# Turning four tiles of a token mixer by VectorE block transposes and DMAs instead of TensorE transposes

## The chip, the cores and the metric

The kernel runs on one core of one Trainium2 chip. The metric is the device time of one execution in microseconds (us), the median over several runs. "Before" is the kernel without the change.

## The reference

Two layers of a decoder trunk act on `x`, 256 tokens of 1024 values, in f32. Each layer is a SwiGLU feed-forward, a mixer with three gated branches, and a second feed-forward, each between two RMS norms. Cut to the mixer, the part that the change touches:

```python
u, bg, cg, q, kv, nsa_g, q_mem, merge_g = jnp.split(h @ w_in, points, axis=-1)
y_conv = bg * short_conv(cg * u, conv_w)                  # 512 channels, width 3 over tokens
...                                                       # y_nsa: native sparse attention
q_m = q_mem.reshape(b, s, MEM_HEADS, MEM_HEAD_DIM)        # 4 heads of 128, 256 memory tokens
s_m = jnp.einsum('bshd,bmhd->bhsm', q_m, mkv[:, :, 0]) * (MEM_HEAD_DIM ** -0.5)
p_m = jax.nn.softmax(s_m, axis=-1)
y_mem = jnp.einsum('bhsm,bmhd->bshd', p_m, mkv[:, :, 1]).reshape(b, s, 512)
g_conv, g_nsa, g_mem = jnp.split(jax.nn.sigmoid(merge_g), 3, axis=-1)
merged = g_conv * (y_conv @ w_br_conv) + g_nsa * (y_nsa @ w_br_nsa) + g_mem * (y_mem @ w_br_mem)
return merged @ w_out
```

## The kernel before

**Streams and steps.** The 256 tokens are two tiles of 128 (`t` = 0 and 1), and each tile is a Python generator, a "stream", that yields after each step of TensorE work. The program runs the two streams in turn, and between them background tasks (attention, compression, memory). A counter `now` counts steps; `later(d, fn)` emits `fn` d steps on. A step of a 512-column projection (`halves`) is six matmuls of 512 columns, and there are 816 steps. The text is thus written in a certain order, and a scheduler then sets the order on each engine from that order, from its table of instruction costs (the lines with `TRN2Spec` change it) and from the buffers that are free; only SP, which issues the weight loads, keeps the order of the text. What an engine got in its list it runs strictly in that order.

**Precision.** Every f32 product is three matmuls in a rounded f32 format: high by high, high by low, low by high. So each weight tile `raw` (128x1024, from a DMA) is split: ACT rounds it to `whi` (L333), DVE subtracts to get `wlo` (L334). Units are split up to `AHEAD` = 4 steps before TensorE needs them, into 8 buffers. Activations are split in the same manner (`evac_split`).

**Turning.** TensorE contracts over partitions, so what a projection leaves as tokens by channels must be turned to channels by tokens before the next one. The kernel has two ways.

- `transpose4` (L441): four TensorE transposes of 128x128 against the identity into one PSUM bank `pt`, which ACT and DVE then read and split. The normed x, the attention's keys and queries, the memory queries `qms`, the convolution's input `v` and gate `bs`, and the gated sum `merged` (in halves of 512 columns) go this way.
- `turn` and `turn_beside`: DVE transposes all 32x32 blocks of a tile (`blocks`, L451), and after `AWAY` = 1 step GpSimd (POOL) issues four DMAs (`moved`, L457) that carry the blocks to their partitions. `wait` steps later ACT and DVE split `moved` (L474, L475). For the block transposes to give the right pieces, the columns are to lie "by lanes", every fourth column together. The feed-forward's gates do it while they read PSUM (`lanes_in`, L661, L663, L668). The SwiGLU products, the attention probabilities, the memory's keys and the memory itself go this way.

**The mixer**, per tile and layer: projections for keys and values, queries, memory queries (`mem_query`), u, C and B (`conv_part`, `conv_out`), then for each branch in `ORDER` = conv, mem, nsa, and for each half n of the 1024 columns: a gate projection whose tanh is `gth`, the branch product `br`, and DVE's gated sum into `merged0` or `merged1` (L1435, L1437, L1438). After the last branch `transpose_half(0)` is emitted `HALF` = 5 steps on, `transpose_half(1)` during the output product `y`, whose unit k takes channels 128k to 128k+127 of the sum; k = 0 to 3 need half 0.

`later(CONV, turn)`, `later(BS, turn)` and `later(QM, turn)` put the transposes of v, bs and qms 7, 4 and 2 steps behind the reads of PSUM. `mem_attention` of both tiles is queued when tile 1's query is turned.

Of the kernel before, what the change touches and what calls it, by code (L numbers as in the profile page):

```python
# [32 lines left out]
P = 128  # L33
# [23 lines left out]
LANES = 4  # L57
NORM_B, NORM_C = 1, 1
AWAY, SPLIT, RETURN = 1, 11, 6
MSTEP, MWAIT = (5, 11), 3  # L60
ABREAST = 6
SECOND_HALF = 1
CONV, BS, CMP, ZC, QS_0, QS_1, QM, PC, YM = 7, 4, 6, 2, 2, 6, 2, 3, 1
ATT_A, ATT_B, ATT_C, ATT_D, ATT_T = 1, 3, 2, 6, 8
EARLY, RAMP, SCALES, STAGED, SETUP = 6, 10, 5, 8, 30
DRAINED = 4
PACE, PACE_1, PACED = 9, 8, ("nsa", "memory")

RUNS = {"ffn1_w_out": 64, "ffn2_w_out": 64, "w_mix_out": 64, "w_branch_conv": 64, "w_branch_mem": 64}
PRE = ("ffn1_norm_pre", "mix_norm_pre", "ffn2_norm_pre", "mem_norm")  # L70
# [73 lines left out]
def f32(ap):  # L144
    return ap.bitcast(F32)
# [19 lines left out]
def program(tc, nc, pools, a, out, plan):  # L165
# [278 lines left out]

    def turn(src, n, finish, wait):
        f = n // 4
        make = gtile if n > 512 else ttile
        blocks = make("blocks")  # L450
        nc.vector.transpose(blocks[:, :n], view(src, 0, [[32, 4], [P, n // P], [1, 32]]))  # L451
        moved = []

        def away():
            moved.append(make("moved"))
            for q in range(4):
                nc.gpsimd.dma_start(moved[0][:, q * f:(q + 1) * f],  # L457
                                    blocks[q * 32:(q + 1) * 32, :n].rearrange("j (p f) -> j p f", p=4))
# [754 lines left out]
    def mem_query(t, l, ps, r):  # L1213
        S = shared[l]
        qs = ttile("qms")
        nc.scalar.activation(qs[:, :512], ps, AF.Copy, scale=r[3])

        def turn():
            pt = transpose4(qs, 0)
            qT = gtile("qmT", F32R)  # L1220
            evac_split(qT[:, 0:512], qT[:, 512:1024], pt)
            S["qm"][t] = qT
            if t == 1:
                S["ymT"] = [gtile("ymemh", F32R), gtile("ymeml", F32R)]
                for u in range(2):
                    add(("memory", l), mem_attention(l, u), True)

        later(QM, turn)

    def mem_attention(l, u):  # L1230
        S = shared[l]
# [49 lines left out]
    def conv_part(t, l, u_s, c_ps, r):  # L1281
        S = shared[l]
        v = ttile("v")
        nc.vector.scalar_tensor_tensor(v[:, :512], c_ps, r[0], u_s[:, :512], op0=OP.mult, op1=OP.mult)
        cT = ttile("cT")

        def turn():
            pt = transpose4(v, 0)
            vT = tp.tile([P, 4, 130], F32, name="vT", tag="tmp")
            if t == 0:  # L1290
                nc.gpsimd.memset(vT[:, :, 0:2], 0.0)
                S["carry"] = sp.tile([P, 4, 2], F32, name="carry", bufs=1)
            else:
                nc.gpsimd.tensor_copy(vT[:, :, 0:2], S["carry"])
            nc.scalar.copy(vT[:, :, 2:130], pt.rearrange("p (c s) -> p c s", c=4))
            if t == 0:
                nc.gpsimd.tensor_copy(S["carry"], vT[:, :, 128:130])
            base = l * 48 + 32
            for c in range(4):
                dst = cT[:, c * P:(c + 1) * P]  # L1300
                w = [convT[:, base + 4 * i + c:base + 4 * i + c + 1] for i in range(3)]
                nc.scalar.activation(dst, pt[:, c * P:(c + 1) * P], AF.Copy, scale=w[2])
# [3 lines left out]
        later(CONV, turn)
        return cT

    def conv_out(cT, b_ps, r, put):
        bs = ttile("bs")  # L1310
        nc.scalar.activation(bs[:, :512], b_ps, AF.Copy, scale=r[1])

        def turn():
            pt = transpose4(bs, 0)
            nc.vector.tensor_tensor(cT[:, :512], cT[:, :512], pt, op=OP.mult)
            y = gtile("yconv", F32R)
            nc.scalar.copy(y[:, 0:512], cT[:, :512])
            nc.vector.tensor_sub(y[:, 512:1024], cT[:, :512], f32(y[:, 0:512]))
            put(y)

        later(BS, turn)

    def branch(yT, name, l, n0):
        ps = bank("br")
# [36 lines left out]
    def mixer(t, l):  # L1361
        S = shared[l]
        hT, r = yield from prenorm(t, "mix_norm_pre", l)

        def columns(c0, n=512):
            return halves(hT, "w_mix_in", l, [(c0, n)])

        ps = yield from columns(2048)
        kv_first(t, l, ps, r)
        ps = yield from halves(hT, "w_mix_in", l, [(2560, P), (2816, 12), (2688, P), (2828, 12)], (0, P, 140, 268))  # L1370
        kv_second(t, l, ps, r)

# [22 lines left out]
        nc.scalar.activation(u_s[:, :512], ps, AF.Copy, scale=r[0])  # L1395
# [4 lines left out]
        conv_out(cT, ps, r, made.append)  # L1400
        merged = [ttile(f"merged{n}") for n in range(2)]
        mh, ml = gtile("mThi", F32R), gtile("mTlo", F32R)

        def transpose_half(n):
            sl = slice(n * 512, (n + 1) * 512)
            evac_split(mh[:, sl], ml[:, sl], transpose4(merged[n], 0))

        for b in ORDER:
            name = ("w_branch_conv", "w_branch_nsa", "w_branch_mem")[b]
            ths = []  # L1410

            def gates(n):
                pg = yield from columns(3352 + b * 1024 + n * 512)
                ths.append(ttile("gth"))
                nc.scalar.activation(ths[n][:, :512], pg, AF.Tanh, scale=r[1])

            if b == 0:
                yield from gates(0)
                yield from gates(1)
            for n in range(2):  # L1420
                if b != 0:
                    yield from gates(n)
                th = ths[n]
# [10 lines left out]
                if b == ORDER[0]:  # L1434
# [89 lines left out]
```

## Time and profile before

| | |
|---|---|
| median of 3 runs (lowest to highest) | 1190.03 us (1189.97 to 1190.53) |
| the profiled execution: its time, its span | 1190.01 us, 1188.3 us |
| granted TensorE clock over the span | 0.999 |
| busy: PE, DVE, ACT, POOL | 1177.2, 891.7, 755.9, 177.2 us |
| TensorE transposes of qms, v, bs, merged | 16, 16, 16, 32 |
| DMAs `moved<-blocks` | 176, 4.3 us from issue to landing for one of 128 KB |
| mixer of layer 0, mixer of layer 1 | about 197 to 421 us, about 788 to 1007 us |

The span runs from the first to the last instruction; 1.7 us of the execution lie outside it. PE is TensorE's matmul side, PEld its weight loads, DVE VectorE, ACT ScalarE, POOL GpSimd. L with a number is a line of the kernel before. A matmul's listed duration runs from its start to its modelled end, and matmuls overlap, so what one costs is read from the distance of starts.

### The profile page before, as it was taken

Reading aid. Unit: us, or ns where it says so; the run is one execution under the profiler, and the core shown is the slowest. Engines: PE = TensorE matmul, PEld = TensorE weight load, DVE = VectorE, ACT = ScalarE, POOL = GpSimd, SP = SyncE. Lnnn points to the kernel's source line nnn. Section 1 sums busy time; section 2 is a strip of 40 time slices with the busy share of each in tenths; the row PEclk is TensorE's granted clock in tenths of the full one; section 3 lists DMA queues with packets and bytes.
Section 4 is the critical chain, followed back from the end, with each engine's and each line's share of the span. In section 5 each row is a group of like instructions: output and inputs, shape, how many; then the busy total and the mean of one; then the engine's idle time right before and its main releaser. Section 6 shows DMA issues by size and latency. Waiting matters only on the chain.

```text
span 1188.3 us, 16619 instructions
## 1 busy us (share of the span) xinstructions
PE 1177.2 (99%) x5777; PEld 1032.5 (87%) x5777; DVE 891.7 (75%) x1130; ACT 755.9 (64%) x1217; POOL 177.2 (15%) x333
## 2 busy tenths in 40 slices
PE   9999999999999999999999999999999999999997
PEld 7888888888988888888888888889888888888886
DVE  6867757798998786676577677588899977767753
ACT  6655836888885565555465565469889655655541
POOL 4001301411120020011011011014012200110100
PEclk9999999999999999999999999999999999999999
DMA  7787875776678767777767678757767687587771
GB/s 258 253 256 240 276 261 154 228 240 192 194 231 216 247 185 221 222 235 230 228 184 230 215 229 270 240 141 242 232 178 229 198 231 229 178 250 213 234 223 63
DMA packets 133764, 260.64 MB, mean 219 GB/s; under 512 B 15694, under 2 KB 36848, under 8 KB 133680
## 3 DMA queue, kind: packets, MB, share of 16 engines
q1 hardware_dynamic: 124048, 235.11, 63.7%
q0 software_dynamic: 9600, 24.47, 7.6%
q8 instruction: 45, 0.74, 0.3%
q14 instruction: 39, 0.32, 0.1%
q10 hardware_dynamic: 32, 0.01, 0.0%
HBM read 235.42 MB, written 2.10 MB: 200 GB/s over the span
## 4 chain that ended last, share of the span: by engine, by line
PE 95%; ACT 2%; DVE 1%; issue 1%; DMA 0%; POOL 0%; SPq 0%; DVEq 0%; POOLq 0%; ACTq 0%
PE acc L410 35%; PE acc L396 9%; PE acc L397 9%; PE acc L398 9%; PE y L398 7%; PE y L396 7%; PE y L397 7%; PE pt L441 2%; PE br L396 2%; PE br L398 2%; PE br L397 2%; ACT whi L333 1%; PE s L1070 1%; DVE wlo L334 0%; PE om L1268 0%
## 5 line engine op out<-in xcount | busy, mean ns | idle before, releaser
L334 DVE TENSOR_TENSOR wlo<-raw,whi 128x1024 fp32r<-128x1024 f32 (+2 forms) x441 | 529.0, 1211 | 186.0 <-ACT whi L333 182.0
L333 ACT CAST whi<-raw 128x1024 fp32r<-128x1024 f32 (+2 forms) x441 | 452.6, 1040 | 255.2 <-PE acc L410 116.1
L457 POOL DMA_DIRECT2D moved<-blocks x176 | 95.8, 563 | 644.6 <-DVE blocks L451 368.9
L410 PE MATMUL acc<-wlo,hThi 128*128 128x512 f32 x640 | 191.6, 380 | 0.0
L410 PE MATMUL acc<-whi,hTlo 128*128 128x512 f32 x640 | 191.4, 380 | 0.0
L410 PE MATMUL acc<-whi,hThi 128*128 128x512 f32 x640 | 191.4, 381 | 0.0
L396 PE MATMUL acc<-whi,hThi 128*128 128x512 f32 (+1 forms) x480 | 182.8, 381 | 0.0
L397 PE MATMUL acc<-wlo,hThi 128*128 128x512 f32 (+1 forms) x480 | 179.3, 374 | 0.3 <-DVE wlo L334 0.2
L398 PE MATMUL acc<-whi,hTlo 128*128 128x512 f32 (+1 forms) x480 | 178.9, 373 | 0.0
L410 PEld LDWEIGHTS acc<-whi,hTlo 128*128 128x128 f32 x640 | 121.2, 189 | 17.3 <-DVE hTlo L513 0.4
L410 PEld LDWEIGHTS acc<-wlo,hThi 128*128 128x128 f32 x640 | 121.1, 189 | 17.0 <-DVE wlo L334 0.3
L410 PEld LDWEIGHTS acc<-whi,hThi 128*128 128x128 f32 x640 | 120.7, 189 | 16.6
L396 PE MATMUL y<-whi,turnhi 128*128 128x512 f32 x352 | 133.8, 380 | 0.0
L397 PE MATMUL y<-wlo,turnhi 128*128 128x512 f32 x352 | 133.7, 380 | 0.0
L398 PE MATMUL y<-whi,turnlo 128*128 128x512 f32 x352 | 133.7, 380 | 0.0
L398 PEld LDWEIGHTS acc<-whi,hTlo 128*128 128x128 f32 x480 | 90.9, 189 | 11.6
L397 PEld LDWEIGHTS acc<-wlo,hThi 128*128 128x128 f32 x480 | 91.1, 190 | 10.9 <-DVE wlo L334 0.9
L396 PEld LDWEIGHTS acc<-whi,hThi 128*128 128x128 f32 x480 | 91.1, 190 | 10.3
L398 PEld LDWEIGHTS y<-whi,turnlo 128*128 128x128 f32 x352 | 66.7, 189 | 9.2
L397 PEld LDWEIGHTS y<-wlo,turnhi 128*128 128x128 f32 x352 | 66.7, 189 | 9.2
L396 PEld LDWEIGHTS y<-whi,turnhi 128*128 128x128 f32 x352 | 66.7, 189 | 9.2
L475 DVE TENSOR_TENSOR turnlo<-moved,turnhi 128x1024 fp32r<-128x1024 f32 (+1 forms) x42 | 49.1, 1168 | 26.8 <-ACT turnhi L474 26.4
(307 smaller groups left out, 1449.6 us busy)
## 6 DMA issues: line engine op xcount, KB each, us to landing
raw<-in_ffn_w_in_dram SPq DMA_DIRECT2D x159, 512.0 KB, 4.7
raw<-in_w_mix_in_dram SPq DMA_DIRECT2D x96, 512.0 KB, 4.5
raw<-in_ffn_w_out_dram SPq DMA_DIRECT2D x88, 512.0 KB, 4.6
moved<-blocks POOLq DMA_DIRECT2D x144, 128.0 KB, 4.3
raw<-in_ffn_w_in_dram SPq DMA_DIRECT2D x34, 256.0 KB, 4.0
raw<-in_w_mem_kv_dram SPq DMA_DIRECT2D x16, 512.0 KB, 4.6
raw<-in_w_mix_out_dram SPq DMA_DIRECT2D x16, 512.0 KB, 4.9
raw<-in_cmp_k_w_dram SPq DMA_DIRECT2D x8, 512.0 KB, 4.6
```

Of the source, the lines that this page charges most:

```text
L333: pinned(nc.scalar.copy(hi[:, c0:c1], raw[:, c0:c1]))
L334: pinned(nc.vector.tensor_sub(lo[:, c0:c1], raw[:, c0:c1], f32(hi[:, c0:c1])))
L396: nc.tensor.matmul(ps, lhsT=xh, rhs=wh, start=start, stop=False, skip_group_check=skip)
L397: nc.tensor.matmul(ps, lhsT=xh, rhs=wl, start=False, stop=False, skip_group_check=skip)
L398: nc.tensor.matmul(ps, lhsT=xl, rhs=wh, start=False, stop=stop, skip_group_check=skip)
L410: pinned(nc.tensor.matmul(ps[j][:, :n], lhsT=hT[x2][:, k], rhs=moving(w, j * n, n), start=(k == 0 and i == 0), stop=(k == 7 and i == 2)))
L441: pinned(nc.tensor.transpose(pt[:, j * P:(j + 1) * P], src[:, c0 + j * P:c0 + (j + 1) * P], ident))
L457: nc.gpsimd.dma_start(moved[0][:, q * f:(q + 1) * f], blocks[q * 32:(q + 1) * 32, :n].rearrange("j (p f) -> j p f", p=4))
L475: nc.vector.tensor_sub(lv, mv, f32(hv))
L1070: nc.tensor.matmul(s3[:, i], lhsT=QT[:, g * 2 + u, i], rhs=pairs(KT[j][:, var * 2 + g], 0, 256), start=(i == 0 and j == 0), stop=(i == 1 a ...
```

## The change

Four tiles change from the first way of turning to the second, and the delays and one cost of the scheduler are set anew.

- **v and bs** (convolution's input and gate): the reads of PSUM (`by_lane`) and the writes put the columns by lanes, `turn(..., laned=True)` transposes blocks on DVE and moves them by four DMAs of 64 KB; the convolution reads `vT`, which ACT copies from `moved`, in place of the PSUM bank; the gate multiplies `moved` instead of `pt`.
- **qms**: `turn_two` writes the block transposes of both tiles into one buffer and moves both with four DMAs of 128 KB, once tile 1's query is there; the split and the start of the memory attention of both tiles follow `QM` steps later.
- **merged, half 0**: tanh, gating and branch product of half 0 are read and written by lanes; after the last branch `move_half` block-transposes it, and the split comes `MERGED` = 11 steps later or ahead of the output product's first unit. Half 1 stays with TensorE.
- **Numbers**: ACT costs 1.05 times as much in the scheduler's table; the constants below.

```diff
+TRN2Spec.CYCLE_T[mybir.EngineType.Activation] *= 1.05
+MERGED = 11
-CONV, BS, CMP, ZC, QS_0, QS_1, QM, PC, YM = 7, 4, 6, 2, 2, 6, 2, 3, 1
-ATT_A, ATT_B, ATT_C, ATT_D, ATT_T = 1, 3, 2, 6, 8
+CONV, BS, CMP, ZC, QS_0, QS_1, QM, PC, YM = 10, 8, 8, 3, 2, 6, 9, 5, 1
+ATT_A, ATT_B, ATT_C, ATT_D, ATT_T = 1, 2, 2, 6, 8
-PACE, PACE_1, PACED = 9, 8, ("nsa", "memory")
+PACE, PACE_1, PACED = 10, 8, ("nsa", "memory")
...
-    def turn(src, n, finish, wait):
+    def turn(src, n, finish, wait, laned=False):
-        nc.vector.transpose(blocks[:, :n], view(src, 0, [[32, 4], [P, n // P], [1, 32]]))
+        nc.vector.transpose(blocks[:, :n], src[:, :n] if laned else view(src, 0, [[32, 4], [P, n // P], [1, 32]]))
...
+    def by_lane(ap, n=512):
+        return view(ap, 0, [[1, 4], [4, n // 4]])
+
+    def turn_two(S, key, t, src, finish, wait):
+        if t == 0:
+            S[key] = gtile("blocks")
+        blocks = S[key]
+        nc.vector.transpose(view(blocks, t * P, [[256, 4], [1, P]]), view(src, 0, [[P, 4], [1, P]]))
+        if t == 0:
+            return
...
+                nc.gpsimd.dma_start(moved[0][:, q * 256:(q + 1) * 256],
+                                    blocks[q * 32:(q + 1) * 32, :].rearrange("j (p f) -> j p f", p=4))
+        later(AWAY, away)
+        later(wait, lambda: finish([view(moved[0], u * P, [[32, 4], [256, 4], [1, 32]]) for u in range(2)]))
...
     # mem_query
-        nc.scalar.activation(qs[:, :512], ps, AF.Copy, scale=r[3])
-            pt = transpose4(qs, 0)
-            evac_split(qT[:, 0:512], qT[:, 512:1024], pt)
-        later(QM, turn)
+        nc.scalar.activation(view(qs, 0, [[P, 4], [1, P]]), by_lane(ps), AF.Copy, scale=r[3])
+                evac_split(quarters(qT[:, 0:512], 4), quarters(qT[:, 512:1024], 4), mv[u])
+        turn_two(S, "qb", t, qs, ready, QM)
...
     # conv_part
-            pt = transpose4(v, 0)
-            nc.scalar.copy(vT[:, :, 2:130], pt.rearrange("p (c s) -> p c s", c=4))
-                nc.scalar.activation(dst, pt[:, c * P:(c + 1) * P], AF.Copy, scale=w[2])
-        later(CONV, turn)
+            nc.scalar.copy(view(vT, 2, [[130, 4], [32, 4], [1, 32]]), mv)
+                nc.scalar.activation(dst, vT[:, c, 2:130], AF.Copy, scale=w[2])
+        turn(v, 512, lambda mv: shifted(mv, t, cT), CONV, True)
...
     # conv_out
-            pt = transpose4(bs, 0)
-            nc.vector.tensor_tensor(cT[:, :512], cT[:, :512], pt, op=OP.mult)
-        later(BS, turn)
+            nc.vector.tensor_tensor(quarters(cT[:, :512], 4), quarters(cT[:, :512], 4), mv, op=OP.mult)
+        turn(bs, 512, lambda mv: gated(mv, cT, put), BS, True)
...
     # mixer
+        def move_half():
+            def place(mv):
+                if not placed:
+                    placed.append(True)
+                    nc.scalar.copy(quarters(mh[:, 0:512], 4), mv)
+                    nc.vector.tensor_sub(quarters(ml[:, 0:512], 4), mv, f32(quarters(mh[:, 0:512], 4)))
+            moved = turn(merged[0], 512, place, MERGED, True)
+            return lambda: place(turned_view(moved[0], 512))
...
+                    if b == 0:
+                        yield ("until", lambda: len(made) > 0)
...
                 if b == ORDER[2] and n == 0:
-                    later(HALF, lambda: transpose_half(0))
+                    first_half = move_half()
...
         def between(k):
+            if k == 0:
+                first_half()
             if k == SECOND:
                 transpose_half(1)
```

Of the built programs' instructions, 64 TensorE transposes go (16 each of qms, v and bs, 16 of the 32 of merged), 16 DVE block transposes come (`STREAM_TRANSPOSE`, four each), and 56 DMAs come on POOL's queue (48 of 64 KB, 8 of 128 KB). The number of ACT instructions stays, and SP's list is the same. The steps of the two streams fall as before.

**TensorE, end of layer 0's mixer.** The half-0 transposes of tile 0's sum stand among the gate products before:

```order
L397 MATMUL acc<-wlo,hThi 128x512
L398 MATMUL acc<-whi,hTlo 128x512
L441 MATMUL pt<-ident,merged_3091 128x128 x4
L396 MATMUL acc<-whi,hThi 128x512
L397 MATMUL acc<-wlo,hThi 128x512
```

and now the gate products go straight over into the output product `y`, with no transposes there:

```order
L399 MATMUL acc<-wlo,hThi 128x512
L400 MATMUL acc<-whi,hTlo 128x512
L398 MATMUL y_4201<-whi,mThi 128x512
L399 MATMUL y_4201<-wlo,mThi 128x512
L400 MATMUL y_4201<-whi,mTlo 128x512
L398 MATMUL y_4202<-whi,mThi 128x512
```

What moved: the four `merged` transposes have left TensorE's list. Between the last matmul of the branch product that completes tile 0's half 0 and the first `y` stand 78 matmuls of 512 columns now.

**DVE, the same place.** Before (from the sum of tile 0's half 0 on; `_3091` and `_3208` are the half-0 sums of tiles 0 and 1):

```order
L1438 TENSOR_TENSOR merged_3091<-merged_3091,gth 128x512
L334 TENSOR_TENSOR wlo<-raw,whi 128x1024 x2
L1437 SCALAR_TENSOR_TENSOR gth<-gth,br 128x512
L1438 TENSOR_TENSOR merged_3208<-merged_3208,gth 128x512
L334 TENSOR_TENSOR wlo<-raw,whi 128x1024 x2
L433 TENSOR_TENSOR mTlo<-pt,mThi 128x512
```

Now (`_3052` and `_3143` are the half-0 sums of the two tiles):

```order
L1477 SCALAR_TENSOR_TENSOR gth<-gth,br 128x512
L1034 TENSOR_TENSOR yf<-o,yf 64x512
L1478 TENSOR_TENSOR merged_3052<-merged_3052,gth 128x512
L336 TENSOR_TENSOR wlo<-raw,whi 128x1024
L1043 TENSOR_TENSOR ynsa<-yf,ynsa 128x512
L453 STREAM_TRANSPOSE blocks<-merged_3052 128x512
L336 TENSOR_TENSOR wlo<-raw,whi 128x1024
L1477 SCALAR_TENSOR_TENSOR gth<-gth,br 128x512
L336 TENSOR_TENSOR wlo<-raw,whi 128x1024
L1478 TENSOR_TENSOR merged_3143<-merged_3143,gth 128x512
L336 TENSOR_TENSOR wlo<-raw,whi 128x1024
L453 STREAM_TRANSPOSE blocks<-merged_3143 128x512
```

What moved: a block transpose of each tile has come in; behind these rows stand one `wlo` and then `mTlo<-moved,mThi` of tile 0, which waits for the four DMAs, with further `wlo` behind it.

**DVE, the convolution of layer 0.** Before, tile 0's `v` is followed by attention work and its turn is TensorE's:

```order
L1284 SCALAR_TENSOR_TENSOR v<-acc,rs,us 128x512
L1192 TENSOR_TENSOR sc<-sc,nmc 128x128
L451 STREAM_TRANSPOSE blocks<-pm 128x1024
L1195 TENSOR_REDUCE smc<-sc 128x8
L334 TENSOR_TENSOR wlo<-raw,whi 128x1024
```

and now:

```order
L1307 SCALAR_TENSOR_TENSOR v<-acc,rs,us 128x512
L435 TENSOR_TENSOR qmT<-moved,qmT 128x512
L453 STREAM_TRANSPOSE blocks<-v 128x512
L1191 TENSOR_TENSOR vlo<-vs,vf 32x64
L1194 TENSOR_TENSOR vst<-vf,gmask 64x128
```

What moved: the memory queries' low parts (`qmT`), before done right after each query, now come here, both tiles together, from `moved`, and `v` has its block transpose on DVE.

More of the change, by code (lines that the diff above doesn't have):

```diff
@@ L465, in turned_view, with away @@
         return view(moved, 0, [[32, n // P], [n // 4, 4], [1, 32]])
+    def by_lane(ap, n=512):
[7 more added lines that the diff above has]
+            return
+        moved = []
+        def away():
+            moved.append(gtile("moved"))
+            for q in range(4):
+                nc.gpsimd.dma_start(moved[0][:, q * 256:(q + 1) * 256],
+                                    blocks[q * 32:(q + 1) * 32, :].rearrange("j (p f) -> j p f", p=4))
+        later(AWAY, away)
+        later(wait, lambda: finish([view(moved[0], u * P, [[32, 4], [256, 4], [1, 32]]) for u in range(2)]))
     def quarters(ap, c):
@@ L1215, in mem_query, with ready @@
         qs = ttile("qms")
-        nc.scalar.activation(qs[:, :512], ps, AF.Copy, scale=r[3])
-        def turn():
-            pt = transpose4(qs, 0)
-            qT = gtile("qmT", F32R)
-            evac_split(qT[:, 0:512], qT[:, 512:1024], pt)
[L1222 to L1226, printed above, removed]
-        later(QM, turn)
+        nc.scalar.activation(view(qs, 0, [[P, 4], [1, P]]), by_lane(ps), AF.Copy, scale=r[3])
+        def ready(mv):
+            for u in range(2):
+                qT = gtile("qmT", F32R)
+                evac_split(quarters(qT[:, 0:512], 4), quarters(qT[:, 512:1024], 4), mv[u])
+                S["qm"][u] = qT
+            S["ymT"] = [gtile("ymemh", F32R), gtile("ymeml", F32R)]
+            for u in range(2):
+                add(("memory", l), mem_attention(l, u), True)
+        turn_two(S, "qb", t, qs, ready, QM)
     def mem_attention(l, u):
@@ L1283, in conv_part, with shifted @@
         v = ttile("v")
-        nc.vector.scalar_tensor_tensor(v[:, :512], c_ps, r[0], u_s[:, :512], op0=OP.mult, op1=OP.mult)
+        lane = lambda ap: view(ap, 0, [[P, 4], [1, P]])
+        nc.vector.scalar_tensor_tensor(lane(v), by_lane(c_ps), r[0], lane(u_s), op0=OP.mult, op1=OP.mult)
         cT = ttile("cT")
-        def turn():
-            pt = transpose4(v, 0)
+        S.setdefault("cT", [None, None])[t] = cT
+        def shifted(mv, t, cT):
             vT = tp.tile([P, 4, 130], F32, name="vT", tag="tmp")
@@ L1301, in turn, with conv_out, gated @@
                 w = [convT[:, base + 4 * i + c:base + 4 * i + c + 1] for i in range(3)]
[L1302 removed]
+                nc.scalar.activation(dst, vT[:, c, 2:130], AF.Copy, scale=w[2])
                 nc.vector.scalar_tensor_tensor(dst, vT[:, c, 1:129], w[1], dst, op0=OP.mult, op1=OP.add)
                 nc.vector.scalar_tensor_tensor(dst, vT[:, c, 0:128], w[0], dst, op0=OP.mult, op1=OP.add)
[L1306 removed]
+        turn(v, 512, lambda mv: shifted(mv, t, cT), CONV, True)
         return cT
[L1309 removed]
+    def conv_out(t, l, cT, b_ps, r, put):
+        S = shared[l]
         bs = ttile("bs")
[L1311 to L1315 removed]
+        nc.scalar.activation(view(bs, 0, [[P, 4], [1, P]]), by_lane(b_ps), AF.Copy, scale=r[1])
+        def gated(mv, cT, put):
+            nc.vector.tensor_tensor(quarters(cT[:, :512], 4), quarters(cT[:, :512], 4), mv, op=OP.mult)
             y = gtile("yconv", F32R)
@@ L1394, in mixer @@
         u_s = ttile("us")
-        nc.scalar.activation(u_s[:, :512], ps, AF.Copy, scale=r[0])
+        nc.scalar.activation(view(u_s, 0, [[P, 4], [1, P]]), by_lane(ps), AF.Copy, scale=r[0])
         ps = yield from columns(1024)
@@ L1399, in mixer @@
         made = []
-        conv_out(cT, ps, r, made.append)
+        conv_out(t, l, cT, ps, r, made.append)
         merged = [ttile(f"merged{n}") for n in range(2)]
@@ L1406, in transpose_half @@
             evac_split(mh[:, sl], ml[:, sl], transpose4(merged[n], 0))
+        placed = []
+        def move_half():
[6 more added lines that the diff above has]
+            return lambda: place(turned_view(moved[0], 512))
         for b in ORDER:
@@ L1414, in gates @@
                 ths.append(ttile("gth"))
-                nc.scalar.activation(ths[n][:, :512], pg, AF.Tanh, scale=r[1])
+                nc.scalar.activation(view(ths[n], 0, [[P, 4], [1, P]]) if n == 0 else ths[n][:, :512],
+                                     by_lane(pg) if n == 0 else pg, AF.Tanh, scale=r[1])
             if b == 0:
@@ L1433, in mixer @@
                 dst = merged[n][:, :512]
-                if b == ORDER[0]:
+                if n == 0:
+                    lane = lambda ap: view(ap, 0, [[P, 4], [1, P]])
+                    if b == ORDER[0]:
+                        nc.vector.scalar_tensor_tensor(lane(dst), lane(th), 1.0, by_lane(pb), op0=OP.add, op1=OP.mult)
+                    else:
+                        nc.vector.scalar_tensor_tensor(lane(th), lane(th), 1.0, by_lane(pb), op0=OP.add, op1=OP.mult)
+                        nc.vector.tensor_add(dst, dst, th[:, :512])
+                elif b == ORDER[0]:
                     nc.vector.scalar_tensor_tensor(dst, th[:, :512], 1.0, pb, op0=OP.add, op1=OP.mult)
```

## The prediction

> **What bounds the kernel.** I read the page's first part, then the chain that ended last, then TensorE's waits, then stretches of the two mixers.
>
> ```profile
> span 1188.3 us, 16619 instructions
> ...
> PE 1177.2 (99%) x5777; PEld 1032.5 (87%) x5777; DVE 891.7 (75%) x1130; ACT 755.9 (64%) x1217; POOL 177.2 (15%) x333
> ...
> PE 95%; ACT 2%; DVE 1%; issue 1%; DMA 0%; POOL 0%; SPq 0%; DVEq 0%; POOLq 0%; ACTq 0%
> ```
>
> TensorE is busy 99% of the span, and 95% of the chain is TensorE's own work, so the time is nearly the sum of what TensorE issues. All its waits over 0.15 us:
>
> ```profile
> PE pt L441 <- DMA x<-in_x_dram: 1.4, 1, 1.4
> PE idle L205 <- DVE idle L200: 1.1, 1, 1.1
> PE z L1111 <- DVE wlo L334: 1.0, 2, 0.6
> PE pt L441 <- POOL kd L905: 0.4, 1, 0.4
> PE z L1109 <- DVE FHL L1100: 0.2, 1, 0.2
> PE acc L397 <- DVE wlo L334: 0.2, 1, 0.2
> ```
>
> The first two belong to the start. Inside a mixer what ends last, when TensorE waits at all, is a late `wlo`, the split of a weight. Where that is near, the stretches show (length, then busy time of PE, PEld, DVE, ACT, POOL); layer 0's mixer first, then layer 1's:
>
> ```profile
> 220.00:260.00 40.00, 38.20 (x228) 32.85 (x227) 35.65 (x47) 36.06 (x67) 14.97 (x21) 1.00 0.79 248
> 260.00:360.00 100.00, 100.00 (x535) 89.05 (x534) 93.52 (x155) 85.45 (x202) 15.73 (x31) 1.00 0.68 206
> 360.00:420.00 60.00, 60.00 (x287) 52.47 (x287) 45.73 (x48) 32.75 (x40) 2.17 (x4) 1.00 0.81 232
> ```
>
> ```profile
> 800.00:860.00 60.00, 59.84 (x363) 53.81 (x362) 51.66 (x72) 54.86 (x129) 15.88 (x24) 1.00 0.76 234
> 860.00:950.00 90.00, 90.00 (x475) 79.94 (x474) 85.89 (x139) 74.12 (x161) 18.73 (x35) 1.00 0.68 202
> ```
>
> TensorE idles 1.80 us in 220 to 260 and 0.16 us in 800 to 860. From 260 to 360 it never idles though DVE is 94% full, and from 360 on DVE has a quarter of its time free. So the mixers have two close seconds: DVE, and early on ACT.
>
> **Removed: 64 TensorE transposes.** Their price is the distance of starts, not the listed duration:
>
> ```profile
> 388.97 0.60 PE L441 MATMUL pt<-ident,merged 128*128 128x128 f32 x4
> 389.33 0.46 PE L396 MATMUL acc<-whi,hThi 128*128 128x512 f32 x1
> 389.63 0.38 PE L397 MATMUL acc<-wlo,hThi 128*128 128x512 f32 x1
> ```
>
> ```profile
> 288.70 0.44 PE pt L441 x4
> ...
> 297.14 0.88 PE pt L441 x8
> ...
> 389.14 0.44 PE pt L441 x4
> ...
> 431.13 95.19 PE acc L410 x441
> ```
>
> In the chain 441 matmuls of 512 columns take 95.19 us, 0.216 each. In the timeline the four transposes hold back the next matmul by 0.36 us, and the matmul behind them takes 0.30 us to the next start in place of 0.216, 0.44 us in all, which is what the chain gives for a set of four (0.88 for eight). Sixteen sets go, all on the path: 16 x 0.44 = 7.04 us. Nothing comes to TensorE's list.
>
> **Added on DVE: 16 block transposes of 512 columns.** No row has that size; the same operation on 1024 and 768 columns, and other operations on 512:
>
> ```profile
> L334 DVE TENSOR_TENSOR wlo<-raw,whi 128x1024 fp32r<-128x1024 f32 x431 | 521.7, 1222 | 184.3 <-ACT whi L333 182.0 <-PE acc L410 1.1
> ...
> L668 DVE TENSOR_TENSOR wide<-th,acc 128x512 f32<-128x512 f32 x40 | 27.5, 688 | 2.9
> L451 DVE STREAM_TRANSPOSE blocks<-wide 128x1024 f32<-128x1024 f32 x16 | 19.8, 1239 | 0.0
> ...
> L451 DVE STREAM_TRANSPOSE blocks<-wide 128x768 f32<-128x768 f32 x8 | 7.8, 975 | 0.1
> ...
> L433 DVE TENSOR_TENSOR mTlo<-pt,mThi 128x512 fp32r<-128x512 f32 x8 | 5.5, 688 | 0.9 <-ACT mThi L432 0.8
> ```
>
> 256 columns less save 0.264 us, so 512 cost about 0.71: 16 x 0.71 = 11.4 us for DVE, four per mixer for v and bs in its full stretch, two for qms ahead of it, two for merged behind it. The splits from `moved` in place of `pt` cost the same. Reading PSUM by lanes is free on DVE: L668 reads `acc` so and takes 688 ns like L433, which doesn't. The same on ACT:
>
> ```profile
> L661 ACT ACTIVATE th<-acc,rs 128x512 f32<-128x512 f32 x40 | 27.4, 685 | 15.5 <-PE acc L410 15.5
> ...
> L578 ACT CAST hThi<-hf 128x512 fp32r<-128x512 f32 x10 | 6.2, 616 | 0.6 <-DVE hf L573 0.6
> ...
> L432 ACT CAST mThi<-pt 128x512 fp32r<-128x512 f32 x8 | 4.7, 586 | 6.9 <-PE pt L441 6.9
> ...
> L1395 ACT ACTIVATE us<-acc,rs 128x512 f32<-128x512 f32 x4 | 2.9, 714 | 0.0
> ```
>
> L661 reads by lanes (685 ns), L1395 straight (714 ns): zero. A copy from SBUF for one from PSUM costs ACT 616 in place of 586 ns, under 1 us over twelve such copies and sixteen of 128 columns: zero.
>
> **Added on POOL: 56 DMAs.**
>
> ```profile
> L457 POOL DMA_DIRECT2D moved<-blocks x176: 541/559/607, 52.6 to 1133.4; - x176
> ...
> DMA to landing us min/median/max: 2.5/4.3/5.9
> ```
>
> ```profile
> L475 DVE TENSOR_TENSOR turnlo<-moved,turnhi 128x1024 fp32r<-128x1024 f32 (+1 forms) x42 | 49.1, 1168 | 26.8 <-ACT turnhi L474 26.4
> ```
>
> ```profile
> ACT turnhi L474 <- DMA moved<-blocks: 33.4, 17, 4.8
> ```
>
> 56 x 0.56 = 31 us on an engine that is busy 177 of 1188; in 260 to 360 it is busy 16 of 100. The queue's order matters more: each set of four is issued in 2.2 us and lands 4.3 us after its issue (64 KB perhaps less; the row is for 128 KB).
>
> The tightest use is half 0 of the sum. By DVE's new order, from the end of the branch product: four operations of 512 columns, one `wlo` (1.22) and the block transpose, 4 x 0.69 + 1.22 + 0.71 = 4.7 us; three issues and the last one's landing, 1.7 + 4.3, to 10.7; ACT's copy 0.6, to 11.3. Meanwhile DVE has four `wlo`, two operations and tile 1's transpose, 7.0 us, to 11.7, and `mTlo` ends at 12.4. TensorE has 78 matmuls until then, 78 x 0.216 = 16.8 us. So it is hidden with 4.4 us to spare. v and bs have more: ten and eight steps of six matmuls, 1.3 us each.
>
> **Added waits.** ACT now waits for landings at four `vT`, four `mThi` and two pairs of `qmT`, DVE at four gate products, and behind the waiting instruction stand `whi` and `wlo`, for which TensorE waits next. L474 has waited 33.4 us over its 42 copies (one for each subtraction of L475), 0.8 us each; I take that. In 260 to 360, DVE: 93.5 + 4 x 0.71 + 0.7 (tile 0's `qmT`, moved here) + 2 x 0.8 = 98.6 us, while TensorE there loses five sets and needs 97.8. That is 0.8 us too much, and the stretch ahead of it leaves nothing in stock (TensorE waits for `wlo` there), so I charge it. In 860 to 950: 85.9 + 2.8 + 1.4 + 1.6 = 91.7 against 90 - 4 x 0.44 = 88.2, 3.5 us too much; but here the stretch ahead has DVE 8 us idle and TensorE all but unheld, so the four steps of splits ahead (`AHEAD`, 4 x 1.3 = 5.2 us) cover it: nothing charged, 3.5 us kept for the upper end. At the lower end the waits in 220 to 260 and 800 to 860 (1.80 + 0.16 us) vanish, since the qms splits leave ACT's and DVE's crowded list there.
>
> The new delays, the pace of the attention and ACT's cost of 1.05 add no instruction; they move others within the mixers. They can shift the same waits either way, and I give them no price beyond those ends.
>
> **Sum.** Profiled execution 1190.0 us (the median of the runs is the same): 1190.0 - 7.04 + 0.8 = 1183.8 us. Ends: 1190.0 - 7.04 - 2.0 = 1181.0 and 1190.0 - 7.04 + 0.8 + 3.5 = 1187.3.
>
> **Rivals.**
>
> *Splits become the bound (slower).* ACT's and DVE's lists are strict, so each landing that is late holds up splits. There are 14 such waits and the longest in the row above is 4.8 us; against them stand 5.2 us of stock. It decides if the waits cost TensorE more than 7.0 + 2.4 = 9.4 us in all, 0.67 each; at 1.0 us each, 1190.0 - 7.0 + 14.0 = 1197. For it: DVE 94 to 95% full. Against: ACT's 33.4 us of such waits before cost TensorE nothing that its own list shows.
>
> *The half of the sum lands late.* If POOL's issues each wait for one DVE subtraction (4 x 1.22 = 4.9 us), the margin of 4.4 turns into 0.5 us of waiting, four times: 1183.8 + 2.0 = 1185.8. Against: 176 issues lie between 541 and 607 ns with DVE busy most of the time, so none was held that long while it ran. The Trainium skill's "SBUF — State Buffer", section "Who interferes with whom", says that a DVE instruction with two SBUF inputs and a GpSimd instruction that reads SBUF shut each other out. The narrow spread of the issues speaks against its bearing on these DMAs.
>
> *No gain where TensorE isn't the bound.* The four sets of qms stand where TensorE waits for splits anyway; if those 1.8 us bring nothing, 1185.6.
>
> *A transpose costs its whole duration.* The row
>
> ```profile
> L441 PE MATMUL pt<-ident,merged 128*128 128x128 f32 x32 | 4.8, 273 | 0.0
> ```
>
> gives 273 ns each: 64 x 0.273 = 17.5 us, so 1172.5. Against: the starts above. The Trainium skill's "TensorE: Matmul & The Clock Gate", section "Part 4: PE-mode transpose", has about 275 ns for a transpose within a kernel; by that the gain would be an estimated 17.6 us. As a duration the trace agrees; as a price it doesn't, 0.11 us by the starts.
>
> **Chances.** Forecast 0.70, no gain at qms 0.10, half late 0.07, whole duration 0.02; splits as the bound 0.06, of which 0.05 end slower; the rest, 0.05, lies between 1187.6 and 1192.4 through a part of those waits. About 0.2% (2.4 us) is what a measurement here tells from no change. Faster 0.88, same 0.07, slower 0.05. The range 1181.0 to 1187.3 holds the forecast, the second and the third and leaves out the rest.
>
> **What would show it.** TensorE: 64 fewer `pt` matmuls, chain still 95% or more TensorE. Block transposes of 512 columns near 0.71 us, DVE's busy time up by about 11 us. No wait of `y` for `mTlo` or `mThi`; `br<-yconv` unheld. TensorE's waits for `wlo` between 240 and 330 up by about 1 us, and near 840 to 950 close to zero. The forecast is wrong if those waits reach several us, or if landings of the small DMAs go well beyond 6 us.

## The result, and the profile after

The changed kernel takes 1183.65 us (median of four runs, 1183.29 to 1184.64), the kernel before, beside it on the same chip, 1190.28 us (1189.97 to 1191.8). The ratio is 0.9943, 95% interval 0.9926 to 0.996: 6.6 us faster, against 6.2 forecast. The profiled execution took 1183.74 us. Line numbers below are those of the kernel they are quoted from; the changed kernel has L333 to L475 of before 2 to 23 lines further down.

The page of the changed kernel: span, busy time, the chain that ended last.

```profile
span 1182.0 us, 16604 instructions
...
PE 1171.0 (99%) x5713; PEld 1024.3 (87%) x5713; DVE 897.4 (76%) x1144; ACT 758.4 (64%) x1217; POOL 203.7 (17%) x389
...
PE 93%; ACT 2%; DVE 2%; issue 1%; DMA 1%; SPq 0%; POOL 0%; DVEq 0%; POOLq 0%; ACTq 0%
```

64 matmuls fewer, and TensorE still 99% busy. The chain counts 93% TensorE, two points less than before.

TensorE's waits from 20 us on, and the stretches that the prediction showed of before (length, then busy time of PE, PEld, DVE, ACT, POOL):

```profile
PE z L1134 <- DVE wlo L336: 0.6, 3, 0.2
PE pt L443 <- POOL kd L928: 0.4, 1, 0.4
PE z L1132 <- DVE FHL L1123: 0.2, 1, 0.2
```

```profile
220.00:260.00 40.00, 38.73 (x228) 33.21 (x226) 36.83 (x50) 36.28 (x73) 17.13 (x23) 1.00 0.79 251
260.00:360.00 100.00, 100.00 (x525) 88.60 (x524) 94.86 (x156) 86.36 (x197) 25.73 (x50) 1.00 0.76 227
360.00:420.00 60.00, 59.92 (x285) 51.78 (x284) 49.64 (x59) 34.36 (x46) 7.05 (x13) 1.00 0.81 245
...
860.00:950.00 90.00, 90.00 (x469) 79.53 (x468) 86.69 (x139) 76.01 (x152) 24.35 (x47) 1.00 0.76 223
```

In 260 to 360 and 860 to 950 TensorE never idles. VectorE has 1.3 us more to do than before in 260 to 360, and 3.9 us more in 360 to 420, where it has room.

The new operations on VectorE and the landings on POOL's queue (KB of one DMA, median us from issue to landing):

```profile
L453 DVE STREAM_TRANSPOSE blocks<-merged 128x512 f32<-128x512 f32 x4 | 2.8, 703 | 0.0
L476 DVE STREAM_TRANSPOSE blocks<-qms 128x512 f32<-128x512 f32 x4 | 2.8, 703 | 0.0
L453 DVE STREAM_TRANSPOSE blocks<-bs 128x512 f32<-128x512 f32 x4 | 2.8, 702 | 0.0
L453 DVE STREAM_TRANSPOSE blocks<-v 128x512 f32<-128x512 f32 x4 | 2.8, 690 | 0.0
...
L1438 DVE TENSOR_TENSOR mTlo<-moved,mThi 128x512 fp32r<-128x512 f32 x4 | 2.8, 689 | 1.2 <-ACT mThi L1437 1.2
```

```profile
moved<-blocks POOLq DMA_DIRECT2D x152, 128.0 KB, 4.4
...
moved<-blocks POOLq DMA_DIRECT2D x48, 64.0 KB, 4.2
```

The first and last starts on TensorE and the last step of VectorE give the length of TensorE's list and of the tail. Before, then after:

```profile
1.12 0.80 PE L205 MATMUL idle<-idle 128*128 128x512 f32 x1 [1.12 <-DVE idle L200]
...
1181.56 0.38 PE L398 MATMUL y<-whi,turnlo 128*128 128x512 f32 x1
...
1183.52 1.42 DVE L625 SCALAR_TENSOR_TENSOR x<-pn,nr,x 128x512 f32<-128x512 f32 x2
```

```profile
1.12 0.80 PE L207 MATMUL idle<-idle 128*128 128x512 f32 x1 [1.12 <-DVE idle L202]
...
1174.61 0.38 PE L400 MATMUL y<-whi,turnlo 128*128 128x512 f32 x1
...
1176.57 1.41 DVE L648 SCALAR_TENSOR_TENSOR x<-pn,nr,x 128x512 f32<-128x512 f32 x2
```

Both lists start at 1.12 us. The last start comes 1181.56 - 1174.61 = 6.95 us earlier, while the span is only 6.3 us shorter: after VectorE's last step the output's store needs 4.0 us here (1182.0 - 1177.98) and 3.3 before (1188.3 - 1184.94).

### The profile page after: what moved, and what is told of

Read it like the earlier page. It is cut to its first block, busy times and chain, and to the rows that moved or that the text cites. A ratio compares the mean times of both kernels' runs of the same rounds, so it can differ in the third digit from the quotient of the medians.

```text
span 1182.0 us, 16604 instructions
## 1 busy us (share of the span) xinstructions
PE 1171.0 (99%) x5713; PEld 1024.3 (87%) x5713; DVE 897.4 (76%) x1144; ACT 758.4 (64%) x1217; POOL 203.7 (17%) x389
## 4 chain that ended last, share of the span: by engine, by line
PE 93%; ACT 2%; DVE 2%; issue 1%; DMA 1%; SPq 0%; POOL 0%; DVEq 0%; POOLq 0%; ACTq 0%
PE acc L412 35%; PE acc L398 9%; PE acc L399 9%; PE acc L400 9%; PE y L398 7%; PE y L399 7%; PE y L400 7%; PE br L400 2%; PE br L398 2%; PE br L399 2%; PE pt L443 1%; ACT whi L335 1%; DVE wlo L336 1%; PE s L1093 1%; DMA raw<-in_w_mix_in_dram 0%
## 5 line engine op out<-in xcount | busy, mean ns | idle before, releaser
L459 POOL DMA_DIRECT2D moved<-blocks x224 | 121.7, 562 | 658.9 <-DVE blocks L453 392.9
```

The source lines that it names most:

```text
L459: nc.gpsimd.dma_start(moved[0][:, q * f:(q + 1) * f], blocks[q * 32:(q + 1) * 32, :n].rearrange("j (p f) -> j p f", p=4))
```

## The experiments

Two questions: is the gain just the places of 64 transposes on TensorE, and what hides the added VectorE work? Twelve kernels were run, each beside the kernel before. In the table, "idle" is TensorE's idle time in the larger part of the two mixers, 350 us less the busy time in 220 to 360 and 800 to 1010 us; gaps below about 0.16 us don't show in it, since listed matmuls overlap (0.38 us long, 0.216 apart). "Mixers" is how long TensorE needs for the two mixers: from the start of the last `y` of the feed-forward ahead of a mixer to the start of the first `y` of the feed-forward behind it, both layers added. It leaves out the start and the end of an execution, which the median holds. Both columns are read from one traced execution of each kernel.

| kernel | median us | ratio to before, 95% | idle us | mixers us |
|---|---|---|---|---|
| before | 1190.28 to 1190.48 | | 2.05 | 665.74 |
| changed | 1183.65 | 0.9943, 0.9926 to 0.996 | 1.36 | 658.35 |
| numbers alone | 1189.72 | 0.9994, 0.9985 to 1.0003 | 1.13 | 665.27 |
| transposes back | 1189.13 | 0.9989, 0.998 to 0.9998 | 1.25 | 664.71 |
| blocks added | 1193.29 | 1.0023, 1.0013 to 1.0033 | 3.09 | 668.65 |
| blocks and numbers | 1190.29 | 1.0001, 0.9993 to 1.001 | 1.36 | 665.40 |
| all numbers back | 1188.97 | 0.9987, 0.9978 to 0.9996 | 5.75 | 664.33 |
| pace back | 1189.10 | 0.999, 0.9981 to 1.0 | 6.00 | 664.84 |
| delays back | 1190.70 | 1.0001, 0.9992 to 1.0009 | 6.16 | 666.11 |
| without ScalarE's 5% | 1183.53 | 0.994, 0.9928 to 0.9953 | 1.94 | 658.63 |
| convolution undone | 1188.99 | 0.999, 0.9981 to 0.9999 | 2.74 | 663.79 |
| queries undone | 1186.72 | 0.9961, 0.9948 to 0.9973 | 1.22 | 660.56 |
| both halves moved | 1184.66 | 0.9953, 0.9941 to 0.9966 | 4.41 | 661.33 |
| both halves, layer 0 | 1185.18 | 0.9957, 0.9944 to 0.9969 | 2.78 | 660.06 |

The idle times come from sums such as these, of before and of the changed kernel:

```profile
sum 350.00, PE 347.95 PEld 307.80 DVE 310.99 ACT 283.27 POOL 65.88; mean PE 173.98 PEld 153.90 DVE 155.50 ACT 141.64 POOL 32.94
```

```profile
sum 350.00, PE 348.64 PEld 307.40 DVE 320.25 ACT 289.48 POOL 92.80; mean PE 174.32 PEld 153.70 DVE 160.12 ACT 144.74 POOL 46.40
```

The marks of the mixers, again of before and of the changed kernel:

```profile
202.41 0.38 PE L398 MATMUL y<-whi,turnlo 128*128 128x512 f32 x1
...
536.51 0.38 PE L396 MATMUL y<-whi,turnhi 128*128 128x512 f32 x1
...
790.56 0.38 PE L398 MATMUL y<-whi,turnlo 128*128 128x512 f32 x1
...
1122.20 0.38 PE L396 MATMUL y<-whi,turnhi 128*128 128x512 f32 x1
```

```profile
202.86 0.38 PE L400 MATMUL y<-whi,turnlo 128*128 128x512 f32 x1
...
533.21 0.38 PE L398 MATMUL y<-whi,turnhi 128*128 128x512 f32 x1
...
787.26 0.38 PE L400 MATMUL y<-whi,turnlo 128*128 128x512 f32 x1
...
1115.26 0.38 PE L398 MATMUL y<-whi,turnhi 128*128 128x512 f32 x1
```

The mixers became 3.75 and 3.64 us shorter, 7.39 together; up to the first mark the changed kernel's execution is 0.45 us behind.

**Numbers alone.** The kernel before with the change's numbers only.

```diff
+TRN2Spec.CYCLE_T[mybir.EngineType.Activation] *= 1.05
-CONV, BS, CMP, ZC, QS_0, QS_1, QM, PC, YM = 7, 4, 6, 2, 2, 6, 2, 3, 1
+CONV, BS, CMP, ZC, QS_0, QS_1, QM, PC, YM = 10, 8, 8, 3, 2, 6, 9, 5, 1
-ATT_A, ATT_B, ATT_C, ATT_D, ATT_T = 1, 3, 2, 6, 8
+ATT_A, ATT_B, ATT_C, ATT_D, ATT_T = 1, 2, 2, 6, 8
-PACE, PACE_1, PACED = 9, 8, ("nsa", "memory")
+PACE, PACE_1, PACED = 10, 8, ("nsa", "memory")
```

> The kernel before with only the change's numbers: ACT's cost of 1.05, the delays, the pace. All 64 transposes stay, no block transpose comes. If the gain is the price of TensorE's transposes (0.44 us for a set of four), this is the time before, 1190.0 within 1.0 us, with TensorE's waits for wlo moved about but of much the same sum. Rival: the new numbers made the gain by a better order around 220 to 260 us; then 1184 to 1186.

1189.72 us, 0.65 below before, and the interval of the ratio, 0.9985 to 1.0003, takes in no difference at all. For the old way of turning, the numbers matter little.

**Transposes back.** The changed kernel, with the 64 transposes issued as well; nothing reads them.

```diff
         turn(v, 512, lambda mv: shifted(mv, t, cT), CONV, True)
+        later(7, lambda: transpose4(v, 0))
...
         turn(bs, 512, lambda mv: gated(mv, cT, put), BS, True)
+        later(4, lambda: transpose4(bs, 0))
...
+        later(2, lambda: transpose4(qs, 0))
...
+                    later(HALF, lambda: transpose4(merged[0], 0))
```

> The changed kernel with the 64 TensorE transposes put back at their old delays, their results unused: the turning still goes by DVE and DMAs. If a set of four costs TensorE 0.44 us and what DVE, ACT and POOL got is hidden, 1183.7 + 16 x 0.44 = 1190.7, 1189.7 to 1191.7. If a transpose costs its listed 273 ns, 1183.7 + 17.5 = 1201. If the new numbers made the gain, about 1184 to 1186.

1189.13 us, 5.5 above the changed kernel and below the expected 1189.7, with hardly a change of idle time (1.25 us). By the medians a set of four costs 0.34 us, where 0.44 was reckoned. By the marks the two mixers are 6.36 us longer, 0.40 a set; the traced executions differ besides in their start (0.3 us) and in the store at the end (0.7 us), where no transpose stands. So the transposes' own places on TensorE are most of the 7.4 us. It is also the end of the rival that took a transpose at its 273 ns: 64 of those are 17.5 us. The Trainium skill's "TensorE: Matmul & The Clock Gate", "Part 4: PE-mode transpose", has about 275 ns for one, in bf16, within a kernel. As the price of one more in TensorE's list this run gives about 0.1 us.

**Blocks added.** The kernel before, old numbers, with the change's 16 block transposes and 56 DMAs issued as well; nothing reads `moved`.

```diff
-        later(CONV, turn)
+        later(CONV, turned)
+        turn(v, 512, lambda mv: None, 10, True)
...
+        turn(bs, 512, lambda mv: None, 8, True)
...
+        turn_two(S, "qb", t, qs, lambda mv: None, 9)
...
+                    turn(merged[0], 512, lambda mv: None, MERGED, True)
```

> The kernel before, with the change's 16 block transposes and 56 DMAs added at their places and nobody reading them: TensorE's list and the splits as before. If the added DVE and POOL work is hidden, 1190.0 to 1190.8, DVE's busy time up by 11 us. Rival, the splits as the bound: DVE is 94 to 95% full in the mixers, 11 us more come through to TensorE by a third or more, 1194 and up.

1193.29 us, 2.9 above before, and by the marks the mixers are 2.91 us longer: not hidden. TensorE's waits got new lines, on things that VectorE and ScalarE finish later:

```profile
PE pt L442 <- DVE phc L1229: 0.6, 1, 0.6
PE acc L411 <- DVE hTlo L601: 0.5, 1, 0.5
...
PE acc L397 <- ACT yf L1031: 0.4, 1, 0.4
```

"TensorE's neighbours have room for 11 us" is thus wrong as a general statement, and the question became why the changed kernel hides the same work.

**Blocks and numbers.** The two kernels above in one.

> The kernel before with both the change's numbers and, beside the TensorE transposes that still feed everything, the change's 16 block transposes and 56 DMAs, whose results nothing uses. The numbers alone gave 1189.7 us, the unused block transposes and DMAs under the old numbers 1193.3. My theory: the old numbers give TensorE's transposes and matmuls too little lead over VectorE once it has some 11 us more to do, and the new ones (a pace of 10, an estimate of ScalarE 5% higher, longer delays) give that lead, so the added work is hidden here: 1189.7 to 1191.0 us, the waits of layer 0's mixer back near 3 us. Rival: what hides the added work in the changed kernel is not the numbers but that the PSUM-read work of the 64 transposes is gone from VectorE and ScalarE with them; then this kernel loses as under the old numbers, 1192.5 to 1194 us.

1190.29 us: hidden, idle 1.36 us as in the changed kernel and the mixers 0.1 us longer than with the numbers alone, although all 64 transposes and their reads of PSUM are there. So the numbers hide the work; the rival, that relief of PSUM reads does it, falls. Nothing waits for the landings in this kernel, so it says nothing of these. And each kernel is one order of the instructions: what an order must have to hide the work, a lead of TensorE or something else, this pair doesn't show.

**All numbers back.** The changed kernel with every number set back that the landings don't need.

```diff
-TRN2Spec.CYCLE_T[mybir.EngineType.Activation] *= 1.05
-CONV, BS, CMP, ZC, QS_0, QS_1, QM, PC, YM = 10, 8, 8, 3, 2, 6, 9, 5, 1
+CONV, BS, CMP, ZC, QS_0, QS_1, QM, PC, YM = 10, 8, 6, 2, 2, 6, 9, 3, 1
-ATT_A, ATT_B, ATT_C, ATT_D, ATT_T = 1, 2, 2, 6, 8
+ATT_A, ATT_B, ATT_C, ATT_D, ATT_T = 1, 3, 2, 6, 8
-PACE, PACE_1, PACED = 10, 8, ("nsa", "memory")
+PACE, PACE_1, PACED = 9, 8, ("nsa", "memory")
```

> The changed kernel with every number that the new path doesn't need set back: ScalarE's estimate without its 5%, CMP 6, ZC 2, PC 3, ATT_B 3, PACE 9 (CONV 10, BS 8, QM 9 and MERGED 11 stay, as the landings need them). If the numbers only matter together with the added VectorE work, this loses 1 to 3 us: 1184.7 to 1186.7 us, in waits of transposes and state matmuls for VectorE or ScalarE between 220 and 360 and between 800 and 950. If they matter nowhere, 1183.2 to 1184.2 us.

1188.97 us: 5.3 lost, more than either expectation, 4.4 of it idle time in the mixers. The largest wait, on the timelines of TensorE, ScalarE and VectorE (idle before an instruction and its releaser in brackets):

```profile
303.68 0.28 PE L399 MATMUL sm<-turnhi,qmT 128*128 128x256 f32 x1
305.47 0.48 PE L1013 MATMUL o<-turnhi,vz 128*128 128x512 f32 x1 [0.43 <-ACT yf L1050]
308.23 0.48 PE L397 MATMUL acc<-whi,hThi 128*128 128x512 f32 x1 [1.63 <-ACT pm L1269]
```

```profile
306.40 0.61 ACT L1317 COPY vT<-moved 128x512 f32<-128x512 f32 x1
307.16 0.47 ACT L1269 ACTIVATE pm<-sm,nmm 128x256 f32<-128x256 f32 x1
```

```profile
304.12 0.68 DVE L1048 TENSOR_TENSOR yf<-oc,yf 64x512 f32<-64x512 f32 x1
304.73 0.69 DVE L452 STREAM_TRANSPOSE blocks<-bs 128x512 f32<-128x512 f32 x1
305.35 1.17 DVE L335 TENSOR_TENSOR wlo<-raw,whi 128x1024 fp32r<-128x1024 f32 x1
306.45 0.67 DVE L1266 TENSOR_REDUCE nmm<-sm 128x2 f32<-128x512 f32 x1
```

The memory's exponential `pm` starts 3.5 us after TensorE's last scores `sm`, and TensorE's next projection, which the listing says waits for it, can't start before. ScalarE is nearly full (busy 11.4 of the 12 us from 296 to 308), but what `pm` waits for is on VectorE (11.8): it needs `nmm`, the negative maximum of the scores, and starts 0.04 us after `nmm` ends. The scores end at 303.96; VectorE takes `nmm` only at 306.45, behind other work in its list, one of the added block transposes (`blocks<-bs`) among it.

**Pace back, without ScalarE's 5%, delays back.** The changed kernel with one group of numbers set back at a time: PACE 9; no factor 1.05; or CMP 6, ZC 2, PC 3 and ATT_B 3.

> The changed kernel with PACE 9 in place of 10 alone: the attention and memory steps start closer together. With all the numbers set back the loss was 5.3 us, of it 4.9 in TensorE's waits in the two mixers, the longest behind ScalarE's exponentials and copies (pm, yf, bs). If the pace carries it: 1186 to 1189 us. If it is the delays or ScalarE's estimate: 1183.2 to 1184.7 us.

> The changed kernel without the 5% on ScalarE's estimate, all else as changed. Since the longest waits with the numbers set back were for ScalarE, an estimate that is too low lets TensorE's steps come too early. If the estimate carries the loss of 5.3 us: 1186 to 1189 us, waits for pm, yf or bs back. If the pace or the delays carry it: 1183.2 to 1184.7 us.

> The changed kernel with CMP 6, ZC 2, PC 3 and ATT_B 3 in place of 8, 3, 5 and 2, all else as changed. If these delays carry the loss of 5.3 us: 1186 to 1189 us, with waits of transposes for pc and of the state's matmuls. If the pace or ScalarE's estimate carry it: 1183.2 to 1184.7 us. Should each of the three numbers' kernels lose about a third, the three act alone and add up; should each lose nearly all, any one of them is needed.

1189.10, 1183.53 and 1190.70 us. The pace and the delays are each needed; ScalarE's factor isn't. The pace alone set back loses 5.45 us, the delays alone 7.05, more than all the numbers together (5.3), so the losses don't add up: the pace and the delays go with one another. One other value of each was run, so whether neighbouring values would do as well stays open. The waits in the mixers differ between the two; pace back first, delays back second:

```profile
PE br L398 <- DVE merged L1475: 2.6, 2, 1.9
PE om L1290 <- DVE yf L1034: 0.8, 2, 0.5
PE br L399 <- DVE wlo L336: 0.8, 1, 0.8
```

```profile
PE acc L398 <- ACT pm L1270: 2.5, 2, 1.4
PE br L398 <- ACT gth L1450: 1.1, 2, 0.6
```

**Convolution undone, queries undone.** The changed kernel with `conv_part`, `conv_out` and the read of u as before (delays 7 and 4), or with `mem_query` as before (delay 2).

> The changed kernel with the convolution's input and gate back on TensorE transposes (eight sets, old delays), the queries and the half sum as changed. At 0.44 us a set 1183.7 + 3.5 = 1187.2, 1186.2 to 1188.2. Rival: the four waits for landings and the block transposes of v and bs stand in DVE's full stretch and cost TensorE about 1 us a layer; then undoing them gives that back and the time is 1185 to 1186.

> The changed kernel with the memory queries transposed on TensorE again (4 sets of four), with their old delay of 2. By the price of a set alone 4 x 0.44 = +1.76 us: 1185.4 us, 1184.9 to 1186.0. When the convolution's part was undone it cost 5.3 us where its 8 sets are 3.5, since TensorE's transposes waited for ScalarE's copy; if that holds for the queries as well, waits of transposes for the queries' copy add 0.5 to 1 us: 1186.0 to 1186.8 us. Rival of the prediction, that this part gains nothing: 1183.2 to 1184.2 us.

Convolution undone: 1188.99 us, 5.3 lost and above the expected range; its eight sets are 3.5 at the prediction's price. A part of the rest stands in TensorE's waits, which the changed kernel does not have:

```profile
PE pt L443 <- ACT bs L1333: 1.1, 1, 1.1
...
PE pt L1227 <- ACT pc L1223: 0.3, 1, 0.3
```

Here the transposes of `bs`, at their old delay of 4 steps, come to the head of TensorE's list before ScalarE has written it. In the changed kernel `bs` goes by DMA, and none of TensorE's waits is for it. Queries undone: 1186.72 us (1184.79 to 1186.95), so the four sets of the queries do bring something, and the rival "no gain at qms" (a kernel without that part as fast as the change) did not occur. The expected waits for the queries' copy are not in the trace. Of the 3.1 us that its traced execution takes longer, 1.6 lie ahead of the first mixer, which the edit doesn't touch: it waits 1.9 us for the first x, where the change's waits 1.4 at the start, and the granted clock of its first 20 us is 0.91, in the changed kernel's trace 1.00. The mixers are 2.21 us longer, so by this trace the part is worth about 2.2 us.

**Both halves moved; both halves, in layer 0 alone.** The changed kernel with half 1 of the sum moved like half 0, its split at the latest ahead of unit 4 of the output product. The edit of the second kernel, cut:

```diff
-                if b == ORDER[2] and n == 0:
-                    first_half = move_half()
+                if b == ORDER[2] and n in laned:
+                    halves_moved.append(move_half(n))
...
-            if k == SECOND:
-                transpose_half(1)
+            if k == 4 and l == 0:
+                halves_moved[1]()
+            if k == SECOND and l == 1:
+                transpose_half(1)
```

> The changed kernel with the second half of the gated sum laid out by lanes and moved by block transposes and DMAs as well, which takes four more sets of four transposes from TensorE (4 x 0.44 us = 1.76 us) and adds 4 block transposes, 16 DMAs. Between the sum's last product and its first use stand 48 to 55 matmuls, 10.4 to 11.9 us of TensorE, and the chain (block transpose 0.7, DMA issues 2.2, landing 4.2 to 6.0, ScalarE copy 0.6 and VectorE subtraction 0.7, with their hand-overs) takes about 11.7 us. So one to four waits of 0 to 1.3 us come for the second half: 1183.0 us, 1181.5 to 1184.5. Rival, that a transfer whose lead is about its own length costs as much as it saves or more, because the matmuls that wait stand in a fixed order with all that is behind them: 1184.5 to 1188 us.

> The changed kernel with the second half of the gated sum moved as well, in layer 0 alone. With both layers the waits of layer 0's mixer stayed at 2.6 us, and all the added waits (3.7 us) were in layer 1's, one of 1.6 us for the moved second half. So here two sets of four transposes go (2 x 0.44 = 0.88 us) and no wait comes: 1182.8 us, 1182.2 to 1183.6. Rival: the changed order moves waits to other places of layer 1, as each change of order here has done: 1184 to 1186 us.

1184.66 and 1185.18 us: neither beats the change, and with these intervals neither is shown to be slower. The traced execution with both layers took 1187.84 us, 3.2 above its kernel's median, so its waits and the last two columns of its row needn't hold for the others. In it one wait of 1.5 us came for the moved half itself, near the expected size, but 1.6 us more in a place that the edit doesn't touch. Layer 0 alone, traced at its median, brought nearly the same there: its mixer of layer 0 is 0.5 us shorter than the changed kernel's, where 0.88 was expected, that of layer 1 is 2.2 us longer. TensorE, ScalarE and VectorE of this kernel:

```profile
958.73 0.43 PE L1016 MATMUL o<-turnlo,vz 128*64 128x512 f32 x1 [0.32 <-DVE turnlo L498]
...
965.29 0.48 PE L400 MATMUL br<-whi,ynsa 128*128 128x512 f32 x1 [1.10 <-DVE ynsa L1043]
```

```profile
956.38 1.04 ACT L497 CAST turnhi<-moved 128x1024 fp32r<-128x1024 f32 x1 [6.04 <-DMA moved<-blocks]
```

```profile
957.45 1.23 DVE L498 TENSOR_TENSOR turnlo<-moved,turnhi 128x1024 fp32r<-128x1024 f32 x1 [3.30 <-ACT turnhi L497]
...
964.55 0.69 DVE L1043 TENSOR_TENSOR ynsa<-yf,ynsa 128x512 fp32r<-128x512 f32 x1
```

and the changed kernel's ScalarE there:

```profile
951.99 1.04 ACT L497 CAST turnhi<-moved 128x1024 fp32r<-128x1024 f32 x1 [0.37 <-DMA moved<-blocks]
```

A landing of layer 1's attention holds ScalarE for 6.0 us in place of 0.4, VectorE behind it for 3.3, and `ynsa` then misses TensorE by 1.1. This is the prediction's slower rival, on a small scale. The last of the four DMAs landed 4.4 us later than in the changed kernel: POOL issued them from 948.66 us on, there from 946.76, and the slowest landing took 6.0 us, there 4.1. The trace names no releaser for the 1.9 us and no reason for the longer landing, so these last links stay open.

## Why the prediction was right, point by point

**64 transposes, -7.04.** TensorE's mixers are 7.39 us shorter, of which 0.69 are less idle time; the other 6.70 are 0.42 us a set. In the other direction they cost 6.36 by the same marks, 5.5 by the medians. The price by distances of starts, 0.44, holds, a little high, and the listed duration is far off.

**16 block transposes, 0.71 us each.** 0.69 to 0.70. VectorE's busy time rose by 5.7 us, though, not 11. The 16 are listed at 11.1 us in all. Of the 5.4 us between, 1.35 are two `yf` operations that have no record in this trace (the page counts 14 more VectorE operations, not 16), all `wlo` together are listed 1.0 us shorter, and 2.5 are more overlap of listed operations (one of 0.70 us at 965.26 has the next behind it at 965.89, 0.63 later).

**Hidden on VectorE.** True of the changed kernel, false as argued. The argument took the mixers' free time as the cover. With the kernel before and the old numbers, the same work cost 2.9 us.

**+0.8 us in 260 to 360.** This term was mis-sized: it measured 0. TensorE never idles there, since VectorE's time there became 94.9 us, not 98.6; the order put 3.9 us more into 360 to 420. In 860 to 950, where 91.7 us were reckoned and 3.5 kept for the upper end, it became 86.7. Instead of adding waits the mixers lost 0.69 us of idle time, in the direction of the prediction's lower end. That the forecast met the profiled execution to 0.1 us is luck: the mixers gained 7.39 us where -7.04 + 0.8 was reckoned, and the other execution's start (0.45 us) and store (0.7 us), to which the prediction gave no change, took the difference back. The kernel without ScalarE's 5%, which turns the same tiles in the same way, has 1181.1 - 1177.76 = 3.3 us there, as before, in a profiled execution of 1182.81 us:

```profile
span 1181.1 us, 16613 instructions
```

```profile
1176.34 1.42 DVE L647 SCALAR_TENSOR_TENSOR x<-pn,nr,x 128x512 f32<-128x512 f32 x2
```

So the new way of turning doesn't bring the longer store with it; two other traces, of both halves moved, have 3.9 us, and how many of the unprofiled runs have it can't be seen.

**The numbers at no price.** This is the step that did not hold. The text said that they "can shift the same waits either way" and gave them nothing. Alone that holds (-0.65 us, within the noise). With the new way of turning they decide: without them it gains 1.5 us (1188.97 against 1190.48 beside it), with them 6.6. The range's upper end, 1187.3, would not have held a kernel with either of the two needed groups left out, and nothing in the argument tells such a kernel from this one. In that the forecast was lucky.

**Tightest use, half 0.** No wait of `y` for `mThi` or `mTlo`; 4.4 us of margin were enough. Half 1, for which the later experiment reckoned no margin, did wait (1.5 us, in the traced execution of both halves moved).

**Chain at 95% or more TensorE.** It is 93%: more of what ends last runs through VectorE, ScalarE and DMAs, while TensorE's idle time fell. The wait for `wlo` in 240 to 330 was to rise by 1 us; it fell from 1.0 to 0.6.

## What to carry to other kernels

When the engine that is the bound runs a fixed list, an instruction taken from it gains its distance of starts (here 0.40 to 0.42 us for a set of four), but in this kernel only with an order in which the other engines' added work is done in time: spare time in a stretch is not yet cover. So price a change and the constants that set the order together, and test them as a two by two table, old and new work against old and new order. A result of either alone (here -0.7 and -1.5 us of -6.6) says little about both.

## What the runs showed of the hardware

DMAs on POOL's queue took as long for 64 KB as for 128 KB, 4.2 against 4.4 us at the median (the rows of landings above), so halving a transfer did not bring its use forward here. The Trainium skill's "DMA: Bandwidth & Descriptors", "Anatomy of one DMA — SWDGE (gpsimd) path", fits 2.0 us plus the bytes at 436 KB per us. By that 64 KB would land in an estimated 2.15 us. The shortest landing of a 64 KB DMA was 2.0 us; the median was twice that. Weights streamed beside these DMAs (mean busy share of the DMA engines 0.76 in 260 to 360); whether that is the reason no run shows.
